# Attention probabilities times values in a fused block: four-pass fp32 products replaced by two fp32r passes for all four heads

## The chip, the cores and the metric

The kernel runs on 1 core of one Trainium2 chip. The metric is the device time of one execution in microseconds (us). The kernel before takes 900.56 us, the median of 3 runs (899.28 to 900.87). From here on TensorE, VectorE, ScalarE, GpSimd and the queue of SyncE are also called PE, DVE, ACT, POOL and SP, as in the profile.

## What is computed

One transformer block on 512 tokens of width 1024, all in float32: a mixer of three attention branches, then attention to a memory of 256 rows, then a gated feed-forward part, each added to the residual. Only the mixer matters here:

```python
o_a = _stick_breaking(q_a, k_a, v_a)                 # 4 heads of 64, each with its own k and v
o_b = _dsa_attention(q_b, k_b, v_b, q_idx, k_idx, w_idx)   # 4 heads share k and v; the best 128 keys of an index score
o_c = _nsa_attention(q_c, k_cmp, v_cmp, k_sel, v_sel, k_win, v_win, gates, ...)  # 4 heads share k and v, three softmaxes
g = jax.nn.sigmoid(p['g_merge'].reshape(B, S, 3, D_MODEL))
merged = g[:,:,0]*(o_a @ w_up[0]) + g[:,:,1]*(o_b @ w_up[1]) + g[:,:,2]*(o_c @ w_up[2])
```

Branch c adds a softmax over 31 compressed keys, one over the selected blocks and one over a window (both are plain causal attention at 512 tokens), each times its gate. Branch b masks the scores by the 128 best of a separate index score and then does one softmax.

## The kernel before

**Precision.** TensorE takes float32 operands as they are, or as "fp32r" in one pass. Nearly every product is written with operands split in two fp32r parts: `split` (line 62) makes `hi` with a cast (ScalarE unless told otherwise) and `lo = src - hi` with a subtraction (VectorE unless told otherwise), and `mm3` (lines 94 to 96) adds three passes. A few small products run on whole float32 operands.

**Order of the work.** The program is written in one order, and a scheduler then sets the order in which each engine gets its instructions, by the place in the program and its own estimates. On the chip each engine keeps to that order, and semaphores hold an instruction until its inputs are there. Weights come in pieces of 512 KB through two rings, both loaded by SP's queue: `load_split` in pool `stage` (three `raw` buffers, `hi` on ACT, `lo` on DVE) and `load_fill` in pool `fill` (two buffers, `lo` on POOL). A ring's piece is loaded when its buffer is free.

**Stages.** First the norm, branch a's projections and stick-breaking attention, beside three of the 24 merge gates (`fill_gate`, `merge_gate`: 24 products of 128x512 for a gate of branch 0 or 2, tile `gf`). Then the projections of b and c, rope, the compressed keys and the index score. Then, in the program's order:

- branch c (`o_c`, lines 625 to 632): for each block `i` of 128 queries `cmp_attention` and two times `rows_attention`; 
- the top-k of the index score: 16 rounds for each of three blocks (`topk_rounds`, lines 615 and 616), on VectorE alone, then the three instructions of line 632 that turn the scores into a mask;
- branch b (`o_b`): `rows_attention` with that mask, so its blocks 1 to 3 can't start before line 632;
- the other five gates of branch 0, `merge_up(0, "a")`, the gates of branch 2, `merge_up(2, "c")`, half of the gates of branch 1, and the rest of the block.

The scheduler puts gates and `merge_up` products between the attention's instructions on TensorE, and rounds of the top-k between those on VectorE.

**One product of probabilities and values** (`apply_v`, lines 561 to 568) takes 128 keys of four heads: four PE transposes of the probabilities into one PSUM bank, one copy to SBUF as float32 (tile `pt`; ACT in branch c, DVE in branch b), and `pair` (line 101): two float32 products, each with the 64 value columns as stationary operand and two heads (256 columns) as moving operand, the first into partitions 0 to 63 and the second into 64 to 127 of `av`. There are 34 such blocks: 4 + 10 + 10 in branch c and 10 in branch b. After each query block the PSUM result is split into `o_hi` and `o_lo` (ACT and DVE, 128x256).

Of the kernel before, what the change touches and what calls it, by code (L numbers as in the profile page):

```python
# [26 lines left out]
def block_kernel(ctx: ExitStack, tc: tile.TileContext, A, out, dbg=None):  # L27
# [16 lines left out]
    cst = const.tile([P, 1408], F32, name="cst")  # L44
    nc.scalar.preload_act_table_set("natural_log_exp_and_others")
    ident = cst[:, 0:128]
    causal = cst[:, 384:896]
    cmpb = cst[:, 896:1024].rearrange("p (h n) -> p h n", n=32)
    rope_t = cst[:, 1024:1536 - 128].rearrange("p (t c d) -> p t c d", t=3, d=32)
# [96 lines left out]
    def cc(c):  # L146
        return slice(c * P, (c + 1) * P)
# [157 lines left out]
    nc.sync.dma_start(cst[:, 128:], A["cst"][:, 128:])  # L305
    nc.vector.memset(fixed[:, 3, :].bitcast(F32), -1.0)
    nc.vector.tensor_copy(fixed[:, 0:3, :], cst[:, 0:384].rearrange("p (a b) -> p a b", b=128))
    flush()
    w0_st.close()

# [118 lines left out]
    vc = bc.tile([32, 64], F32, name="vc")  # L429
# [68 lines left out]
    def compressed(hid):  # L498
        hs = cw.tile([P, 512], F32, name="rel", bufs=2)
        v, t = hs[0:32, 0:256], hs[0:32, 256:512]  # L500
        nc.scalar.copy(v, hid[0:32].rearrange("p a b -> p (a b)"))
        nc.vector.tensor_mul(t, v, v)
        nc.vector.tensor_scalar(t, t, 0.044715, 1.0, op0=ALU.mult, op1=ALU.add)
        nc.vector.tensor_mul(t, t, v)
        nc.scalar.activation(t, t, AF.Exp, scale=-1.5957691216057308)
        nc.vector.tensor_scalar(t, t, 1.0, None, op0=ALU.add)
        nc.vector.reciprocal(t, t)
        nc.vector.tensor_mul(v, v, t)
        tp = ps.tile([P, 512], F32, name="ps")
# [60 lines left out]
    def rows_attention(i, q, k, v, bias, gate, o_ps, first, last, eng=nc.scalar):  # L570
        n = (i + 1) * P
        pr = mq.tile([P, 4, 512], F32, name="pr", bufs=2)
        nm = mq.tile([P, 4], F32, name="nm", bufs=2)
        den = mq.tile([P, 4], F32, name="den", bufs=2)
        for h in range(4):
            st = gm_ps.tile([P, 512], F32, name="gm")
            scores(st[:, :n], q[:, h, cc(i)], [t[:, 0:n] for t in k])
            nc.vector.tensor_tensor_reduce(pr[:, h, :n], st[:, :n], bias, -1.0, 3e38, ALU.add, ALU.min, nm[:, h:h + 1])
            nc.scalar.activation(pr[:, h, :n], pr[:, h, :n], AF.Exp, bias=nm[:, h:h + 1], scale=-1.0, accum_out=den[:, h:h + 1])
        sc = mq.tile([P, 4], F32, name="sc", bufs=2)  # L580
        nc.vector.reciprocal(sc, den)
        if gate is not None:
            nc.vector.tensor_mul(sc, sc, gate)
        for h in range(4):
            if eng is nc.scalar:
                nc.scalar.activation(pr[:, h, :n], pr[:, h, :n], AF.Copy, scale=sc[:, h:h + 1])
            else:
                nc.vector.tensor_scalar(pr[:, h, :n], pr[:, h, :n], sc[:, h:h + 1], None, op0=ALU.mult)
        for j in range(i + 1):
            apply_v(o_ps, v[:, j, :], pr[:, :, cc(j)], first and j == 0, last and j == i, eng=eng)  # L590

    def cmp_attention(i, o_ps, first, last):
        s = mq.tile([P, 4, 32], F32, name="cs")
# [12 lines left out]
        sc = mq.tile([P, 4], F32, name="sc", bufs=2)
        nc.vector.reciprocal(sc, den)
        nc.vector.tensor_mul(sc, sc, gates[:, i, 0::3])
        nc.vector.tensor_mul(s, s, sc.unsqueeze(2).to_broadcast([P, 4, 32]))
        apply_v(o_ps, vc, s, first, last, k=32)  # L610

    def topk_rounds(i, n):
        for _ in range(n):
            m8 = mq.tile([P, 8], F32, name="m8", bufs=3)
            nc.vector.max(m8, score[i])
            nc.vector.match_replace(score[i], m8, score[i], -3e38)

    o_c = o_pair("c", mq)
    for i in range(NT):
        o_ps = av_ps.tile([P, 2, P], F32, name="av")  # L620
        cmp_attention(i, o_ps, True, False)
        rows_attention(i, qc, ksel, vs["vsel"], causal_bias(i), gates[:, i, 1::3], o_ps, False, False)
        rows_attention(i, qc, kwin, vs["vwin"], causal_bias(i), gates[:, i, 2::3], o_ps, False, True)
# [7 lines left out]
    for i in range(1, NT):  # L631
        nc.vector.tensor_scalar(score[i], score[i], -2e38, NEG, op0=ALU.is_gt, op1=ALU.mult)
    o_b = o_pair("b", op)
    for i in range(NT):
        o_ps = av_ps.tile([P, 2, P], F32, name="av")
        rows_attention(i, qb, kb, vs["vb"], score[i] if i else causal_bias(0), None, o_ps, True, True, nc.vector)
        split(o_b[0][:, :, cc(i)], o_b[1][:, :, cc(i)], o_ps, scale=0.5)
    dump("o_b", o_b[0].bitcast(F32))
    for f in range(early_g, NK):
        fill_gate(0, f)  # L640
# [240 lines left out]
def constants():  # L881
    import numpy as np

    c = np.zeros((128, 1408), np.float32)
    i = np.arange(128)
    c[:, 0:128] = np.eye(128, dtype=np.float32)
    c[:, 128:256] = np.where(i[:, None] >= i[None, :], -1.0, 0.0)
    c[:, 256:384] = np.where(i[:, None] >= i[None, :], NEG, 0.0)
    c[:, 768:896] = np.where(i[None, :] > i[:, None], NEG, 0.0)
    n = np.arange(32)  # L890
    for t in range(4):
        q = t * 128 + i
        c[:, 896 + 32 * t:928 + 32 * t] = np.where((16 * n[None, :] + 31 <= q[:, None]) & (n[None, :] < 31), 0.0, NEG)
# [32 lines left out]
```

## Time and profile before

| | |
|---|---|
| median of 3 runs | 900.56 us (899.28 to 900.87) |
| the profiled execution itself | 898.28 us |
| its span, first to last instruction | 896.5 us |
| PE / PE weight load / DVE / ACT / POOL busy | 856.3 / 731.7 / 507.8 / 411.5 / 140.7 us |
| mean granted clock of TensorE | 0.994 |
| branch c with the top-k | 196.7 to 267.0 us |
| branch b | 267.0 to 300.8 us |

Matmuls are pipelined: one is listed with a length of 0.40 us while the next starts 0.23 us later, so the cost of a product is read from start to start. VectorE's instructions overlap by some 0.08 us in the same way. A float32 product appears as two matmuls in the trace, so a block of `pair` is four of them. A row with x12 merges twelve instructions that follow each other.

### The profile page before, as it was taken

The numbers are of one execution on the slowest core, as the hardware profiler recorded it, in microseconds if no ns is written. First come the engines' busy times: TensorE is split into PE (matmuls) and PEld (weight loads), VectorE is DVE, ScalarE is ACT, GpSimd is POOL, SyncE is SP. The second block draws the span as 40 slices with busy tenths as digits, with TensorE's granted clock in tenths as the row PEclk, the third lists the DMA queues.
The fourth block names the chain that finished last, engine by engine and source line by source line (L and its number), as shares of the span: only waits on it lengthen the run. The fifth ranks groups of instructions, "written<-read, shape, count | busy, mean of one in ns | idle before, by whom it ended". The sixth has DMA issues, their size and how long they took to land.

```text
span 896.5 us, 13084 instructions
## 1 busy us (share of the span) xinstructions
PE 856.3 (96%) x5012; PEld 731.7 (82%) x5012; DVE 507.8 (57%) x1155; ACT 411.5 (46%) x779; POOL 140.7 (16%) x116
## 2 busy tenths in 40 slices
PE   5999999899989999999989999999999999999995
PEld 5987899787757788978878979988888888888884
DVE  4456378799998305676677758643443334322226
ACT  6487545557774224544654545432322333211123
POOL 4021232302211347430232010000000000000002
PEclk9999999999999999999999999999999999999998
DMA  9340124510210334558446514642333332333312
GB/s 323 85 110 24 43 58 119 141 48 24 70 26 24 95 94 141 187 174 246 125 150 199 165 49 142 187 142 94 97 102 105 97 94 94 118 94 95 99 42 94
DMA packets 93710, 99.00 MB, mean 110 GB/s; under 512 B 4656, under 2 KB 81616, under 8 KB 93648
## 3 DMA queue, kind: packets, MB, share of 16 engines
q1 hardware_dynamic: 91568, 92.75, 34.0%
q10 hardware_dynamic: 2080, 5.42, 1.9%
q8 instruction: 39, 0.64, 0.3%
q14 instruction: 23, 0.19, 0.1%
HBM read 96.06 MB, written 2.10 MB: 109 GB/s over the span
## 4 chain that ended last, share of the span: by engine, by line
PE 85%; DVE 7%; ACT 4%; issue 2%; DMA 1%; POOL 0%; ACTq 0%; DVEq 0%; POOLq 0%
PE wo L95 9%; PE wo L96 9%; PE wo L94 9%; PE gf L94 6%; PE gf L95 6%; PE gf L96 6%; PE ff L94 4%; PE ff L95 4%; PE ff L96 4%; PE gm L94 3%; PE gm L95 3%; PE gm L96 3%; PE y L96 2%; PE y L94 2%; PE y L95 2%; PE av L101 2%
## 5 line engine op out<-in xcount | busy, mean ns | idle before, releaser
L58 ACT CAST whi<-raw 128x1024 fp32r<-128x1024 f32 (+1 forms) x167 | 174.8, 1048 | 292.4 <-PE y L96 78.9
L66 DVE TENSOR_TENSOR wlo<-raw,whi 128x1024 fp32r<-128x1024 f32 (+1 forms) x131 | 164.1, 1255 | 211.2 <-ACT whi L58 210.9
L66 POOL TENSOR_TENSOR wlo<-raw,whi 128x1024 fp32r<-128x1024 f32 x36 | 88.9, 2474 | 312.9 <-ACT whi L58 267.1
L95 PE MATMUL wo<-ut_lo,whi 128*128 128x256 f32 (+1 forms) x320 | 105.2, 329 | 0.0
L96 PE MATMUL wo<-ut_hi,wlo 128*128 128x256 f32 (+1 forms) x320 | 104.6, 327 | 0.0
L94 PE MATMUL wo<-ut_hi,whi 128*128 128x256 f32 (+1 forms) x320 | 104.4, 326 | 0.0
L96 PE MATMUL gf<-ut_hi,wlo 128*128 128x512 f32 (+1 forms) x192 | 69.8, 363 | 0.0
L94 PE MATMUL gf<-ut_hi,whi 128*128 128x512 f32 (+1 forms) x192 | 69.3, 361 | 0.0
L95 PE MATMUL gf<-ut_lo,whi 128*128 128x512 f32 (+1 forms) x192 | 69.3, 361 | 0.0
L94 PE MATMUL ff<-ut_hi,whi 128*128 128x512 f32 (+1 forms) x192 | 67.9, 354 | 0.0
L95 PE MATMUL ff<-ut_lo,whi 128*128 128x512 f32 (+1 forms) x192 | 67.9, 354 | 0.0
L96 PE MATMUL ff<-ut_hi,wlo 128*128 128x512 f32 (+1 forms) x192 | 67.9, 354 | 0.0
L95 PEld LDWEIGHTS wo<-ut_lo,whi 128*128 128x128 f32 x320 | 60.9, 190 | 6.2 <-issue 1.0
L94 PEld LDWEIGHTS wo<-ut_hi,whi 128*128 128x128 f32 x320 | 60.8, 190 | 5.8 <-issue 0.7
L96 PEld LDWEIGHTS wo<-ut_hi,wlo 128*128 128x128 f32 x320 | 60.8, 190 | 5.6 <-issue 0.4
L875 POOL TENSOR_TENSOR ut_hi<-ut_hi,ut_lo 128x512 f32<-128x512 f32 x4 | 5.0, 1276 | 367.0 <-ACT ut_hi L874 367.0
L94 PE MATMUL gm<-whi,ut_hi 128*128 128x256 f32 (+1 forms) x160 | 47.4, 296 | 0.0
L95 PE MATMUL gm<-wlo,ut_hi 128*128 128x256 f32 (+1 forms) x160 | 46.4, 290 | 0.0
L96 PE MATMUL gm<-whi,ut_lo 128*128 128x256 f32 (+1 forms) x160 | 46.3, 289 | 0.0
L96 PEld LDWEIGHTS gf<-ut_hi,wlo 128*128 128x128 f32 x192 | 36.2, 188 | 5.6 <-issue 1.2
L95 PEld LDWEIGHTS gf<-ut_lo,whi 128*128 128x128 f32 x192 | 36.2, 188 | 5.4 <-issue 0.8
L94 PEld LDWEIGHTS gf<-ut_hi,whi 128*128 128x128 f32 x192 | 36.2, 188 | 5.3 <-issue 0.8
(329 smaller groups left out, 2027.7 us busy)
## 6 DMA issues: line engine op xcount, KB each, us to landing
raw<-in_w_ffn_in_dram SPq DMA_DIRECT2D x56, 512.0 KB, 3.6
raw<-in_w_in_dram SPq DMA_DIRECT2D x46, 512.0 KB, 3.9
raw<-in_w_ffn_out_dram SPq DMA_DIRECT2D x22, 512.0 KB, 3.5
raw<-in_w_out_dram SPq DMA_DIRECT2D x16, 512.0 KB, 3.6
raw<-in_w_up_dram SPq DMA_DIRECT2D x8, 512.0 KB, 4.0
xt<-in_x_dram SPq DMA_DIRECT2D x4, 512.0 KB, 9.0
raw<-in_w_mem_kv_dram SPq DMA_DIRECT2D x4, 512.0 KB, 3.8
raw<-in_w_mem_q_dram SPq DMA_DIRECT2D x4, 512.0 KB, 3.8
```

Source lines behind the costliest of these rows:

```text
L58: nc.scalar.copy(dst, src)
L66: (lo_eng or nc.vector).tensor_sub(dst_lo, src, dst_hi.bitcast(F32))
L94: nc.tensor.matmul(dst, lh, rh, start=first, stop=False, skip_group_check=True)
L95: nc.tensor.matmul(dst, lh, rl, start=False, stop=False, skip_group_check=True)
L96: return nc.tensor.matmul(dst, ll, rh, start=False, stop=last, skip_group_check=True).ins
L101: nc.tensor.matmul(dst[64 * x:64 * x + 64], lhs[x], rhs[x], start=first, stop=last, skip_group_check=True)
L875: nc.gpsimd.tensor_mul(yo[:, n], yo[:, n], gain[:, n])
```

## The change

1. `apply_v` turns the transposed probabilities into two fp32r parts (`pt_hi` by ACT, `pt_lo` by DVE, both from PSUM, 128x512) instead of one float32 copy, in both branches. The values stand as 128 stationary columns, their high part beside their low part, and two products, `pt_hi` and `pt_lo`, each 512 columns wide (four heads), add into one PSUM bank. So partitions 0 to 63 of `av` hold the high value part's result and 64 to 127 the low part's.
2. `fold` adds the two halves after each query block: two ACT copies (64x256) into a `raw` buffer of the `stage` ring, two DVE additions (64x256), then the split into `o_hi` and `o_lo` from SBUF.
3. `two_parts` splits the values of the three row attentions once (128x256, ACT and DVE each).
4. `cmp_attention` has no buffer of its own any more: it takes one of the two `pr` buffers of the row attentions, GpSimd clears columns 32 to 127 of it, and its transposes and product run over 128 keys.
5. The table of constants is laid out anew, and the rope tables are loaded later, into a pool of the projections. The program's order of attention and gates is as before.

```diff
-    def apply_v(o_ps, v, src, first, last, k=P, eng=nc.scalar):
+    def apply_v(o_ps, v, src, first, last):
         tp = ps.tile([P, 4, P], F32, name="ps")
         for h in range(4):
-            nc.tensor.transpose(tp[0:k, h, :], src[:, h, :], ident)
-        pt = mq.tile([P, 4, P], F32, name="pt", bufs=3)
-        copy(eng, pt[0:k], tp[0:k])
-        pair(o_ps, [v, v], [pt[0:k, x::2, :] for x in range(2)], first, last)
+            nc.tensor.transpose(tp[:, h, :], src[:, h, :], ident)
+        pt = [mq.tile([P, 4, P], F32R, name=n, bufs=2) for n in ("pt_hi", "pt_lo")]
+        split(pt[0], pt[1], tp)
+        for x in range(2):
+            nc.tensor.matmul(o_ps, v.rearrange("p a d -> p (a d)"), pt[x].rearrange("p h q -> p (h q)"),
+                             start=first and x == 0, stop=last and x == 1, skip_group_check=True)
+
+    def fold(o, i, o_ps):
+        ov = o_ps.rearrange("p (a b q) -> p a b q", a=2, b=2)
+        hi, lo = (t[:, :, cc(i)] for t in o)
+        t = stage.tile([P, WT], F32, name="raw", bufs=3)[:, 0:2 * P].rearrange("p (a q) -> p a q", a=2)
+        top, bot = slice(0, 64), slice(64, 128)
+        nc.scalar.copy(t[top], ov[bot, :, 0, :])
+        nc.scalar.copy(t[bot], ov[top, :, 1, :])
+        nc.vector.tensor_add(t[top], ov[top, :, 0, :], t[top])
+        nc.vector.tensor_add(t[bot], ov[bot, :, 1, :], t[bot])
+        split(hi, lo, t, scale=0.5)
...
     def cmp_attention(i, o_ps, first, last):
-        s = mq.tile([P, 4, 32], F32, name="cs")
+        pr = mq.tile([P, 4, 512], F32, name="pr", bufs=2)
+        s = pr[:, :, 0:32]
+        nc.gpsimd.memset(pr[:, :, 32:128], 0.0)
...
-        apply_v(o_ps, vc, s, first, last, k=32)
+        apply_v(o_ps, vc, pr[:, :, 0:128], first, last)
...
+    def two_parts(v):
+        t = mq.tile([P, NT, 2, 64], F32R, name="v2", bufs=2)
+        split(t[:, :, 0, :], t[:, :, 1, :], v)
+        return t
+
+    vsel, vwin = two_parts(vs["vsel"]), two_parts(vs["vwin"])
...
-        o_ps = av_ps.tile([P, 2, P], F32, name="av")
+        o_ps = av_ps.tile([P, 512], F32, name="av")
...
-        split(o_c[0][:, :, cc(i)], o_c[1][:, :, cc(i)], o_ps, scale=0.5)
+        fold(o_c, i, o_ps)
...
+    rope_t = pw.tile([P, 3, NT, 32], F32, name="rope_t")
+    nc.sync.dma_start(rope_t, A["cst"][:, 1024:1408].rearrange("p (t c d) -> p t c d", t=3, d=32))
```

How the scheduler's order changes, at three places.

VectorE in branch c, in the last query block. `score_1246` to `score_1248` (before) and `score_1250` to `score_1252` (changed) are the three index scores, `m_...` the eight maxima of a round. Before:

```order
L615 MAX m_3298<-score_1248 128x8
L615 MAX m_3301<-score_1246 128x8
L616 MATCH_REPLACE score_1248<-m_3298,score_1248 128x512
L616 MATCH_REPLACE score_1246<-m_3301,score_1246 128x256
L581 RECIPROCAL sc<-den 128x4
L615 MAX m_3304<-score_1247 128x8
L583 TENSOR_TENSOR sc<-sc,gates 128x4
L615 MAX m_3307<-score_1248 128x8
```

Changed:

```order
L637 MATCH_REPLACE score_1252<-m_3356,score_1252 128x512
L65 TENSOR_TENSOR pt_lo<-ps,pt_hi 128x512 x2
L636 MAX m_3359<-score_1250 128x8
L636 MAX m_3362<-score_1251 128x8
L65 TENSOR_TENSOR pt_lo<-ps,pt_hi 128x512
L600 RECIPROCAL sc<-den 128x4
L637 MATCH_REPLACE score_1250<-m_3359,score_1250 128x256
L65 TENSOR_TENSOR pt_lo<-ps,pt_hi 128x512
```

All 24 `pt_lo` subtractions of branch c, all eight additions of its `fold`, four `o_lo` (before: three) and two of the `two_parts` stand between the first instruction of the compressed attention and the first mask instruction; of the 96 top-k instructions all but one stand ahead of the mask, as all did before.

VectorE just ahead of the attention (`wlo` is a weight piece of `load_split`; the one here belongs to a gate of branch 1, which is multiplied behind the attention). Before:

```order
L66 TENSOR_TENSOR wlo<-raw,whi 128x1024
L66 TENSOR_TENSOR stk<-t_2570,stk 128x4x64
L66 TENSOR_TENSOR kc_lo<-ps,kc_hi 128x32
L522 COPY vc<-ps 32x64
L615 MAX m_3184<-score_1246 128x8
```

Changed:

```order
L65 TENSOR_TENSOR stk<-t_2576,stk 128x4x64
L65 TENSOR_TENSOR kc_lo<-ps,kc_hi 128x32
L65 TENSOR_TENSOR vc<-ps,vc 32x64
L636 MAX m_3269<-score_1250 128x8
```

Two such pieces (the other is half of `w_up` of branch c) stood among the last 15 instructions ahead of the attention; both now come after it.

TensorE at the end of the attention (`vb` before and `v_3418` now are branch b's values, `o_hi`/`o_lo` beside `whi`/`wlo` are `merge_up`, `ut_hi`/`ut_lo` are gates). Before:

```order
L101 MATMUL av<-pt,vb 64x256 x4
L96 MATMUL gf<-ut_hi,wlo 128x512
L94 MATMUL gf<-ut_hi,whi 128x512
L565 MATMUL ps<-cst,pr 128x128 x4
L95 MATMUL gf<-ut_lo,whi 128x512
L565 MATMUL ps<-cst,pr 128x128 x3
L101 MATMUL av<-pt,vb 64x256 x6
L565 MATMUL ps<-cst,pr 128x128 x5
L96 MATMUL gf<-ut_hi,wlo 128x512
L94 MATMUL gf<-ut_hi,whi 128x512
L101 MATMUL av<-pt,vb 64x256 x8
```

Changed:

```order
L574 MATMUL av<-pt_hi,v_3418 128x512
L95 MATMUL gf<-o_hi,wlo 128x512
L93 MATMUL gf<-o_hi,whi 128x512
L94 MATMUL gf<-o_lo,whi 128x512
L95 MATMUL gf<-o_hi,wlo 128x512
L574 MATMUL av<-pt_lo,v_3418 128x512
L93 MATMUL gf<-o_hi,whi 128x512
L94 MATMUL gf<-o_lo,whi 128x512
```

28 of the 512-column products (13 of gates, 6 of `merge_up(0)`, 9 of `merge_up(2)`) that stood ahead of the last probability-value product stand behind it now. From branch c's first score to branch b's first score TensorE's order holds 128 of them (110 before), and from there to the last probability-value product 30 (70 before).

## Rows read from the trace of the kernel before

**Rows 1.** The page: busy time of each engine.

```profile
PE 856.3 (96%) x5012; PEld 731.7 (82%) x5012; DVE 507.8 (57%) x1155; ACT 411.5 (46%) x779; POOL 140.7 (16%) x116
```

**Rows 2.** Busy time by stretch: start:end, length, each engine's busy us, granted clock, DMA.

```profile
core 0: us, PE busy (x) PEld busy (x) DVE busy (x) ACT busy (x) POOL busy (x), PEclk, DMA share, GB/s
180.20:196.70 16.50, 16.50 (x125) 15.21 (x125) 15.22 (x42) 9.52 (x20) 0.00 (x0) 1.00 0.19 48
196.70:267.00 70.30, 67.92 (x402) 48.70 (x401) 67.92 (x261) 54.66 (x137) 11.94 (x5) 1.00 0.13 36
267.00:300.80 33.80, 31.05 (x171) 22.59 (x167) 26.09 (x78) 13.27 (x38) 4.75 (x2) 0.95 0.16 45
300.80:896.50 595.70, 577.40 (x3142) 494.09 (x3142) 287.71 (x450) 224.23 (x344) 79.80 (x46) 0.99 0.40 124
```

**Rows 3.** Timeline of VectorE, end of the top-k: start, length, instruction.

```profile
266.41 0.68 DVE L616 MATCH_REPLACE8 score<-m,score 128x512 f32<-128x512 f32 x1
267.00 0.55 DVE L632 TENSOR_SCALAR score<-score 128x256 f32<-128x256 f32 x2
```

**Rows 4.** Groups of VectorE from 190 to 310 us: busy us, mean ns, idle before.

```profile
L60 DVE COPY pt<-ps 128x512 f32<-128x512 f32 x10 | 6.6, 687 | 3.1 <-PE av L101 2.2 <-PE ps L565 0.9
L388 DVE SCALAR_TENSOR_TENSOR g<-g,gf 128x512 f32<-128x512 f32 x8 | 5.5, 682 | 2.4 <-PE gf L96 2.4
L69 DVE SCALAR_TENSOR_TENSOR o_lo<-av,o_hi 128x256 fp32r<-128x256 f32 x8 | 3.4, 421 | 2.2 <-ACT o_hi L68 2.0
```

**Rows 5.** Timeline of VectorE in the first norm: a 128x512 subtraction from PSUM.

```profile
10.17 0.68 DVE L66 TENSOR_TENSOR ut_lo<-ps,ut_hi 128x512 fp32r<-128x512 f32 x1
10.77 1.21 DVE L66 TENSOR_TENSOR wlo<-raw,whi 128x1024 fp32r<-128x1024 f32 x1
```

**Rows 6.** Timeline of VectorE ahead of the attention.

```profile
190.50 1.21 DVE L66 TENSOR_TENSOR wlo<-raw,whi 128x1024 fp32r<-128x1024 f32 x1
191.63 0.41 DVE L66 TENSOR_TENSOR stk<-t,stk 128x256 fp32r<-128x256 f32 x1
```

**Rows 7.** Timeline of TensorE around three probability-value products.

```profile
234.46 0.39 PE L96 MATMUL gf<-ut_hi,wlo 128*128 128x512 f32 x1
234.78 1.52 PE L101 MATMUL av<-pt,vsel 128*64 128x256 f32 x12
236.22 0.50 PE L94 MATMUL gf<-ut_hi,whi 128*128 128x512 f32 x1
236.56 0.40 PE L95 MATMUL gf<-ut_lo,whi 128*128 128x512 f32 x1
236.79 0.40 PE L96 MATMUL gf<-ut_hi,wlo 128*128 128x512 f32 x1
```

**Rows 8.** Busy time in pieces of 2.5 us around the dip of the granted clock.

```profile
265.00:267.50 2.50, 1.50 (x11) 0.51 (x7) 2.50 (x8) 0.81 (x2) 0.36 (x1) 1.00 0.36 82
267.50:270.00 2.50, 1.29 (x5) 1.29 (x6) 2.23 (x11) 1.27 (x6) 0.00 (x0) 0.73 0.43 128
270.00:272.50 2.50, 2.50 (x10) 2.12 (x10) 2.01 (x11) 1.48 (x7) 0.00 (x0) 0.59 0.00 0
```

**Rows 9.** Timeline of TensorE inside that dip.

```profile
270.16 0.63 PE L95 MATMUL gf<-o_lo,whi 128*128 128x512 f32 x1
270.59 0.41 PE L292 MATMUL gm<-kb_hi,qi 128*128 128x256 f32 x1
```

**Rows 10.** Groups of ScalarE from 190 to 310 us.

```profile
L58 ACT COPY pt<-ps 128x512 f32<-128x512 f32 x20 | 10.7, 586 | 4.3 <-PE ps L565 3.3 <-PE ps L293 0.9
L68 ACT ACTIVATE o_hi<-av 128x256 fp32r<-128x256 f32 x8 | 3.1, 384 | 9.8 <-PE av L101 9.8
```

**Rows 11.** Timeline of TensorE at the last probability-value product.

```profile
298.69 2.10 PE L101 MATMUL av<-pt,vb 128*64 128x256 f32 x16
300.72 0.50 PE L95 MATMUL gf<-ut_lo,whi 128*128 128x512 f32 x1
```

**Rows 12.** Group of GpSimd from 196 to 345 us.

```profile
L66 POOL TENSOR_TENSOR wlo<-raw,whi 128x1024 fp32r<-128x1024 f32 x15 | 35.8, 2388 | 123.4 <-ACT whi L58 110.4 <-PE gf L96 13.0
```

More of the change, by code (lines that the diff above doesn't have):

```diff
@@ L43, in block_kernel @@
     utp = pool(ctx, "ut")
-    cst = const.tile([P, 1408], F32, name="cst")
+    cst = const.tile([P, 768], F32, name="cst")
     nc.scalar.preload_act_table_set("natural_log_exp_and_others")
     ident = cst[:, 0:128]
-    causal = cst[:, 384:896]
-    cmpb = cst[:, 896:1024].rearrange("p (h n) -> p h n", n=32)
-    rope_t = cst[:, 1024:1536 - 128].rearrange("p (t c d) -> p t c d", t=3, d=32)
+    causal = cst[:, 128:640]
+    cmpb = cst[:, 640:768].rearrange("p (h n) -> p h n", n=32)
     eps = const.tile([P, 1], F32, name="eps")
@@ L304, in block_kernel @@
             project_chunk(c, 256, w_a[8 * i:8 * i + 8], post)
-    nc.sync.dma_start(cst[:, 128:], A["cst"][:, 128:])
+    tri = pw.tile([P, 2, 128], F32, name="tri")
+    nc.sync.dma_start(tri, A["cst"][:, 768:1024].rearrange("p (a b) -> p a b", b=128))
+    nc.sync.dma_start(cst[:, 128:], A["cst"][:, 128:768])
     nc.vector.memset(fixed[:, 3, :].bitcast(F32), -1.0)
-    nc.vector.tensor_copy(fixed[:, 0:3, :], cst[:, 0:384].rearrange("p (a b) -> p a b", b=128))
+    nc.vector.tensor_copy(fixed[:, 0, :], ident)
+    nc.vector.tensor_copy(fixed[:, 1:3, :], tri)
     flush()
@@ L428, in block_kernel @@
     kc = k_pair(bc, "kc", 32)
-    vc = bc.tile([32, 64], F32, name="vc")
+    vc = bc.tile([P, 2, 64], F32R, name="vc")
+    nc.gpsimd.memset(vc.bitcast(F32), 0.0)
     score = [None] + [bc.tile([P, (i + 1) * P], F32, name=f"score{i}") for i in range(1, NT)]
@@ L521, in compressed @@
         split(kc[0], kc[1], res[:, 0:32])
-        nc.vector.tensor_copy(vc, res[0:32, 64:128])
+        split(vc[0:32, 0, :], vc[0:32, 1, :], res[0:32, 64:128])
     project([(1732, 256)], 4, post_g2)
@@ L589, in rows_attention @@
         for j in range(i + 1):
-            apply_v(o_ps, v[:, j, :], pr[:, :, cc(j)], first and j == 0, last and j == i, eng=eng)
+            apply_v(o_ps, v[:, j, :, :], pr[:, :, cc(j)], first and j == 0, last and j == i)
     def cmp_attention(i, o_ps, first, last):
-        s = mq.tile([P, 4, 32], F32, name="cs")
+        pr = mq.tile([P, 4, 512], F32, name="pr", bufs=2)
+        s = pr[:, :, 0:32]
+        nc.gpsimd.memset(pr[:, :, 32:128], 0.0)
         st = ps.tile([P, 4, P], F32, name="ps")
@@ L616, in topk_rounds @@
             nc.vector.match_replace(score[i], m8, score[i], -3e38)
+    def two_parts(v):
[3 more added lines that the diff above has]
+    vsel, vwin = two_parts(vs["vsel"]), two_parts(vs["vwin"])
     o_c = o_pair("c", mq)
     for i in range(NT):
-        o_ps = av_ps.tile([P, 2, P], F32, name="av")
+        o_ps = av_ps.tile([P, 512], F32, name="av")
         cmp_attention(i, o_ps, True, False)
-        rows_attention(i, qc, ksel, vs["vsel"], causal_bias(i), gates[:, i, 1::3], o_ps, False, False)
-        rows_attention(i, qc, kwin, vs["vwin"], causal_bias(i), gates[:, i, 2::3], o_ps, False, True)
-        split(o_c[0][:, :, cc(i)], o_c[1][:, :, cc(i)], o_ps, scale=0.5)
+        rows_attention(i, qc, ksel, vsel, causal_bias(i), gates[:, i, 1::3], o_ps, False, False)
+        rows_attention(i, qc, kwin, vwin, causal_bias(i), gates[:, i, 2::3], o_ps, False, True)
+        fold(o_c, i, o_ps)
     dump("o_c", o_c[0].bitcast(F32))
@@ L633, in block_kernel @@
     o_b = o_pair("b", op)
+    vb = two_parts(vs["vb"])
     for i in range(NT):
-        o_ps = av_ps.tile([P, 2, P], F32, name="av")
-        rows_attention(i, qb, kb, vs["vb"], score[i] if i else causal_bias(0), None, o_ps, True, True, nc.vector)
-        split(o_b[0][:, :, cc(i)], o_b[1][:, :, cc(i)], o_ps, scale=0.5)
+        o_ps = av_ps.tile([P, 512], F32, name="av")
+        rows_attention(i, qb, kb, vb, score[i] if i else causal_bias(0), None, o_ps, True, True, nc.vector)
+        fold(o_b, i, o_ps)
     dump("o_b", o_b[0].bitcast(F32))
@@ L886, in constants @@
     c[:, 0:128] = np.eye(128, dtype=np.float32)
-    c[:, 128:256] = np.where(i[:, None] >= i[None, :], -1.0, 0.0)
-    c[:, 256:384] = np.where(i[:, None] >= i[None, :], NEG, 0.0)
-    c[:, 768:896] = np.where(i[None, :] > i[:, None], NEG, 0.0)
+    c[:, 768:896] = np.where(i[:, None] >= i[None, :], -1.0, 0.0)
+    c[:, 896:1024] = np.where(i[:, None] >= i[None, :], NEG, 0.0)
+    c[:, 512:640] = np.where(i[None, :] > i[:, None], NEG, 0.0)
     n = np.arange(32)
@@ L892, in constants @@
         q = t * 128 + i
-        c[:, 896 + 32 * t:928 + 32 * t] = np.where((16 * n[None, :] + 31 <= q[:, None]) & (n[None, :] < 31), 0.0, NEG)
+        c[:, 640 + 32 * t:672 + 32 * t] = np.where((16 * n[None, :] + 31 <= q[:, None]) & (n[None, :] < 31), 0.0, NEG)
     inv = np.float32(10000.0) ** (-np.arange(0, 64, 2, dtype=np.float32) / np.float32(64))
```

## Prediction

> **What bounds the kernel now.** On the page TensorE is busy 856.3 us and VectorE 507.8 [rows 1], which makes TensorE look like the one limit. So I next read the busy times by stretch [rows 2], because an edit in the attention is worth what that stretch makes of it. In the 70.3 us of branch c with the top-k, VectorE is busy 67.92 us, exactly as long as TensorE: both are full, and VectorE has 2.4 us to spare. In branch b (33.8 us) TensorE has 31.05 and VectorE 26.09. Behind it TensorE is busy for 577.4 of 595.7 us. Then I looked at what ends branch c: the mask instruction at 267.00 stands on VectorE right behind the last replacement of the top-k [rows 3], and branch b's blocks 1 to 3 cannot begin before it. In a stretch with two full engines, work taken from one gains nothing when work is given to the other, and this change does that.
>
> **What it does to TensorE.** Three blocks of the old float32 product run from 234.78 to 236.22, so one takes 0.48 us [rows 7]. A 512-column fp32r product takes 0.23 (236.56 to 236.79), and the new block is two, 0.46: over 34 blocks 0.7 us. More comes from the borders: before a float32 group the gap is 0.32 and behind it 0.34 instead of 0.23 [rows 7], 0.2 a group, and TensorE's old order has 20 groups: 4 us. So at most 4.7 us leave TensorE. Twelve transposes more stand ahead of branch b's first score; at no more than the 0.23 of a product four times as wide they are 2.8 us at most, and TensorE's waits found below cover them. The Trainium skill, "FP8 and Floating Point Precision", section "TensorE Precision Notes", says that true fp32 takes 4 passes through the array. By that rule, an estimate, one half of the old block is 4 x 256 columns at 2.4 GHz, 0.43 us, and both halves in turn 0.85, so that 34 blocks would give back 13 us; the 0.48 us of the row, which covers both halves, does not bear that out, and the sum goes by the row.
>
> **What it does to VectorE in branch c.** From the order, between the first compressed-attention instruction and the mask:
> - 24 subtractions `pt_lo` are new (the copies they go with were ScalarE's). The nearest row is a subtraction of the same 128x512 shape from PSUM: 0.68 long, and the next instruction starts 0.60 after it [rows 5]. 24 x 0.60 = 14.4 us.
> - 8 `fold` additions of 64x256; the nearest row is `o_lo`, 256 elements a partition, 0.42 long [rows 4], less the same 0.08 overlap 0.34: 2.7 us.
> - one `o_lo` and two `two_parts` more, 0.34 each: 1.0 us.
> - one replacement moves behind the mask: 267.00 less 266.41 [rows 3], -0.6 us.
>
> Sum +17.5 us on an engine that has 2.4 free. Ahead of the stretch two `wlo` leave, 1.13 us each from start to start (190.50 to 191.63) [rows 6]; VectorE is busy 15.22 of the 16.5 us there, but so is TensorE [rows 2], so I take 2.0 of the 2.3. The mask then comes at 267.0 - 2.0 + 17.5 = 282.5 if VectorE waits as little as before. It now also waits for ScalarE's cast before each subtraction, and the compressed attention waits for a `pr` buffer and for GpSimd's clearing, which is queued behind `wlo` pieces of 2.4 us [rows 12]: 0 to 5 us, I take 2, since the top-k rounds between them still fill most gaps, as they do now. Mask at 284.5. TensorE cannot set a longer time: 67.9 us, plus 18 more 512-column products (4.1) and the transposes (2.8), is 75 us at most, against VectorE's 85.4.
>
> **Branch b.** On VectorE the ten copies become ten subtractions (0.69 against 0.68, nothing). Two `merge_up` instructions (-1.2) and four `o_lo` (-1.4) go behind the stretch; six additions (+2.0), one `two_parts` (+0.3) and the replacement (+0.6) come in: 26.1 + 0.3 = 26.4 us. TensorE loses 40 of its 70 products of 512 columns, 9.2 us. So the stretch, 33.8 us now, is no shorter than 27, and no longer than the 34 it takes with the larger TensorE load; I take 30, since some of VectorE's 7.7 idle us stood behind those products (`pt` waited 3.1 and `g` 2.4 [rows 4]).
>
> **Behind the attention.** The last probability-value product ends at 300.7 now [rows 11] and would end at 284.5 + 30 = 314.5, 13.7 us later. 28 products, 28 x 0.23 = 6.4 us, that ran before it now come after it. From there TensorE is full, so both are added.
>
> **What costs nothing.** ScalarE gets ten casts of 0.59 and sixteen copies of at most 0.38 [rows 10] over both stretches, 12 us, beside 67.9 busy of 104 [rows 2]; uncovered, they would stand in the chain of a block, which the 5 us above bound. The rope table leaves SP's queue when branch a has ended and is read some microseconds later; its 0.2 MB is less than half of a weight piece, and I count 0. On SP's queue the two `w_up` pieces of branch c now wait for `raw` buffers that `fold` holds, and hold later pieces back; four gates' pieces stand ahead of them, 24 x 0.23 = 5.5 us of TensorE each, which cover it. Without that cover the wait of a piece would show, and one gate's 5.5 us bounds it.
>
> **The sum.** -2.0 + 17.5 + 2.0 - 3.8 + 6.4 = +20.1 us. The profiled execution took 898.28, 2.28 under the median of the runs, so it would become 918.4, and the median 900.56 + 20.1 = 920.7. With no added waits and branch b at 27 it is +15.1 (915.7); with 5 us of waits and 34 it is +27.1 (927.7).
>
> **Rivals.**
> - *TensorE's clock falls.* Around 265 to 270 us, with TensorE busy 1.50 and 1.29 of 2.5 us, the granted clock went to 0.73 and 0.59, that is to the lower of its two levels (1.2 instead of 2.4 GHz) for most of 5 us [rows 8], and a 512-column product took 0.43 us from start to start [rows 9]. In the changed branch c TensorE would be busy 75 of 87 us at most, so dips are likely. If it spent more than a fifth of that at the lower level, its 75 us (x 1.87 there) would pass VectorE's 87 and set the time: a third gives 75 x 1.29 = 97, 10 us more, 930. Against: at 1.50 of 2.5 us, 60%, it was still granted 1.00 [rows 8], and 75 of 87 is 86%. The Trainium skill, "TensorE: Matmul & The Clock Gate", section "What's actually happening", makes this the rule, a TensorE that goes idle falls back to half rate; the dip agrees with it, at 0.59.
> - *TensorE alone sets the pace (faster).* If the top-k were mere filling and its end did not hold up branch b, the 17.5 us would vanish in gaps and the 4.7 us of TensorE would come off: 895.9. That needs more than 17.5 us of VectorE idle ahead of the mask, and rows 2 show 2.4; for it speaks only that TensorE is just as busy.
> - *Only part is exposed.* If the mask came no later than TensorE's own additions make it (4.1 + 2.8 - 3 of borders, about 4 us), the sum is -2 + 4 - 3.8 + 6.4 = +4.6: 905.2. It would take most subtractions in places where VectorE now waits. In its mild form the change can't be told from none.
> - *That the attention's place before the gates is not changed* is settled by the order: the 28 products did move.
>
> **How the numbers follow.** The forecast, VectorE sets branch c, has 0.72 and its own range 916 to 928; the clock 0.10 at 927 to 940; partly exposed 0.10 at 900 to 910; faster 0.08. The time predicted is the forecast's, 920.7. The range reaches up to 932, into the clock's case, and down to 910, so that the two low cases and a bit of the clock, just under 0.2, are left out. About 0.2% (1.8 us) is what a measurement can tell from no change: faster 0.08 (the second rival), same 0.03 (part of the third), slower 0.89.
>
> **What would show it.** Right: VectorE at 95% or more from 195 to about 285 with the mask near 284; TensorE with waits for `pt_lo` or for VectorE's maxima there, in all some 20 us more idle than the 5 of the two stretches now; subtractions of 0.68 on VectorE; the last product near 314, and from there to the end some 602 us. Wrong: a mask before 275, or TensorE busy as fully as now through branch c; products of 0.43 us over long parts of it mean the first rival.

## The result and the profile after

The changed kernel takes 924.01 us, the median of 4 runs (923.13 to 925.62); the kernel before took 899.92 (898.47 to 900.87) beside it. The ratio is 1.0271, 95% interval 1.025 to 1.0292: slower, inside the predicted range and 3.3 us above the predicted time. The profiled execution has a span of 923.8 us against 896.5.

The page of the changed kernel, busy times and the slices of three engines and the clock, stands against [rows 1]:

```profile
PE 864.4 (94%) x4944; PEld 741.7 (80%) x4944; DVE 533.6 (58%) x1199; ACT 423.3 (46%) x809; POOL 141.2 (15%) x121
PE   5999999899974899999999999999999999999995
DVE  4466388799989820847678676653443344322226
PEclk9999999999986999999999999999999999999998
```

VectorE has 25.8 us more, TensorE 8.1. TensorE was 96% busy and is 94%. Its row has one hole, the 12th to 14th slice (254 to 323 us), which read 7, 4 and 8; in the deepest of them, the 13th (277 to 300 us), VectorE's row reads 9. By stretch (start:end, length, busy us of PE, PEld, DVE, ACT, POOL, granted clock), with the end of TensorE's branch c and the mask as borders, to be laid beside [rows 2]:

```profile
195.60:276.90 81.30, 73.74 (x360) 55.72 (x359) 76.63 (x261) 57.83 (x146) 13.24 (x8) 0.96 0.12 33
276.90:288.40 11.50, 0.00 (x0) 0.00 (x0) 11.44 (x35) 1.15 (x3) 0.00 (x0) 0.58 0.00 0
288.40:319.30 30.90, 25.70 (x119) 19.34 (x120) 26.82 (x82) 17.88 (x49) 2.41 (x1) 0.88 0.16 52
319.30:923.80 604.50, 585.35 (x3171) 500.54 (x3169) 295.18 (x460) 229.90 (x353) 80.50 (x47) 0.99 0.41 127
```

Branch c with the top-k took 70.3 us and now takes 92.8, the first two rows together. VectorE is busy for 88.07 of them, 95%. TensorE is busy for 73.74, has finished its last product of branch c at 276.9, and then does nothing at all until VectorE is through. The span's 27.3 us are -1.1 (the stretch starts at 195.6 instead of 196.7), +22.5 (branch c), -2.9 (branch b, 30.9 instead of 33.8) and +8.8 (behind the attention, 604.5 instead of 595.7).

TensorE's timeline over the hole (start, length, instruction, in brackets the idle time and what ended it), and of VectorE's the last maximum ahead of the mask, the first mask instruction, and the first row maximum behind the mask:

```profile
274.63 0.78 PE L574 MATMUL av<-pt_lo,v 128*128 128x512 f32 x1
275.65 0.50 PE L574 MATMUL av<-pt_hi,v 128*128 128x512 f32 x1 [0.25 <-ACT pt_hi L57]
276.38 0.50 PE L574 MATMUL av<-pt_lo,v 128*128 128x512 f32 x1 [0.23 <-DVE pt_lo L65]
290.62 0.47 PE L291 MATMUL gm<-kb_hi,qi 128*128 128x128 f32 x1 [13.74 <-DVE nm L597]
```

```profile
287.77 0.68 DVE L636 MAX8 m<-score 128x8 f32<-128x512 f32 x1
288.38 0.27 DVE L659 TENSOR_SCALAR score<-score 128x256 f32<-128x256 f32 x1
290.26 0.29 DVE L597 CUSTOM_DVE_ANT_0 pr<-gm,cst 128x128 f32<-128x128 f32 x1
```

The mask instruction, at 267.00 before [rows 3], starts at 288.38. TensorE's next score product needs a PSUM buffer that VectorE's row maximum of branch b's first block sets free (290.26), and that maximum is queued behind the top-k and the mask: 13.74 us of waiting, in one piece. The first block itself needs no mask; it is VectorE's order that holds it up. No run moved this maximum ahead of the top-k. Where VectorE's time went, by groups of the stretch from 195.6 to 288.4 (busy us, mean ns, idle before):

```profile
L65 DVE TENSOR_TENSOR pt_lo<-ps,pt_hi 128x512 fp32r<-128x512 f32 x24 | 15.9, 683 | 1.9 <-ACT pt_hi L57 1.9
L621 DVE TENSOR_SCALAR nm<-nm 128x4 f32<-128x4 f32 x4 | 2.2, 548 | 0.0
L586 DVE TENSOR_TENSOR raw<-av,raw 64x256 f32<-64x256 f32 x4 | 1.7, 427 | 0.1
L585 DVE TENSOR_TENSOR raw<-av,raw 64x256 f32<-64x256 f32 x4 | 1.6, 411 | 0.0
```

The 24 new subtractions are by far the largest group that was not there before. The second row is a surprise, told at the end.

### The profile page after: what moved, and what is told of

Same layout as the page of the kernel before. It is cut to its first block, busy times and chain, and to the rows that moved or that the text cites. A ratio compares the mean times of both kernels' runs of the same rounds, so it can differ in the third digit from the quotient of the medians.

```text
span 923.8 us, 13054 instructions
## 1 busy us (share of the span) xinstructions
PE 864.4 (94%) x4944; PEld 741.7 (80%) x4944; DVE 533.6 (58%) x1199; ACT 423.3 (46%) x809; POOL 141.2 (15%) x121
## 4 chain that ended last, share of the span: by engine, by line
PE 77%; DVE 13%; ACT 4%; DMA 3%; issue 2%; POOL 0%; ACTq 0%; DVEq 0%; SPq 0%; POOLq 0%
PE wo L94 8%; PE wo L95 8%; PE wo L93 8%; PE gf L93 5%; PE gf L94 5%; PE gf L95 5%; PE ff L94 4%; PE ff L93 4%; PE ff L95 4%; PE gm L93 2%; PE gm L94 2%; PE gm L95 2%; PE y L93 2%; PE y L95 2%; PE y L94 2%
## 5 line engine op out<-in xcount | busy, mean ns | idle before, releaser
L93 PEld LDWEIGHTS ff<-ut_hi,whi 128*128 128x128 f32 x192 | 36.3, 189 | 5.0
L95 PEld LDWEIGHTS ff<-ut_hi,wlo 128*128 128x128 f32 x192 | 36.3, 189 | 5.0
L94 PEld LDWEIGHTS ff<-ut_lo,whi 128*128 128x128 f32 x192 | 36.3, 189 | 4.9
```

What stands on the lines that cost most here:

```text
L93: nc.tensor.matmul(dst, lh, rh, start=first, stop=False, skip_group_check=True)
L94: nc.tensor.matmul(dst, lh, rl, start=False, stop=False, skip_group_check=True)
L95: return nc.tensor.matmul(dst, ll, rh, start=False, stop=last, skip_group_check=True).ins
```

## The experiments

Theory V is the prediction's: VectorE's sum of work sets the time of the mask, and TensorE loses what it waits for. Against it stood W, that the time goes on TensorE's own new product blocks and their dependences, whatever VectorE does, and T, the prediction's first rival, that the clock is the loss. All were timed in 3 rounds beside the kernel before; the medians of the kernel before were 899.64 for the first four, then 898.0, 899.07 and 899.3.

| run | edit | median us | ratio, 95% | mask at |
|---|---|---|---|---|
| changed kernel | none | 924.01 | 1.0271 (1.025 to 1.0292) | 288.4 |
| 1 | changed, no low part | 905.19 | 1.0057 (1.0037 to 1.0077) | 271.0 |
| 3 | changed, 8 rounds of top-k | 898.96 | 0.999 (0.9981 to 1.0) | 244.3 |
| 4 | before, 8 rounds of top-k | 896.09 | 0.9969 (0.9953 to 0.9985) | 234.9 |
| 5 | before, 20 subtractions added | 911.96 | 1.0139 (1.0123 to 1.0154) | 281.8 |
| 2a | changed, gates and a merge moved ahead | 920.96 | 1.0245 (1.0222 to 1.0268) | 286.7 |
| 2b | before, gates and a merge moved ahead | 900.54 | 1.0031 (1.0019 to 1.0043) | 267 |
| 6 | changed, low part on GpSimd | 930.66 | 1.0359 (1.0341 to 1.0377) | 283.7 |
| 7 | 6 and 2a together | 928.01 | 1.0324 (1.0303 to 1.0346) | 286.2 |
| 8 | changed, 8 gates ahead, no merge | 904.42 | 1.0061 (1.0046 to 1.0076) | 285.5 |
| 11 | changed, 9 gates ahead, no merge | 898.29 | 0.9993 (0.9983 to 1.0003) | 286.7 |
| 9 | changed, 13 gates ahead, no merge | 909.12 | 1.0115 (1.01 to 1.013) | 286.2 |
| 10 | before, 8 gates ahead, no merge | 893.74 | 0.9943 (0.9926 to 0.9959) | 266.3 |

### Less and more work on VectorE (runs 1, 3, 4, 5)

Run 1 takes the low part of the probabilities away from the changed kernel, on VectorE and on TensorE:

```diff
-        pt = [mq.tile([P, 4, P], F32R, name=n, bufs=2) for n in ("pt_hi", "pt_lo")]
-        split(pt[0], pt[1], tp)
-        for x in range(2):
+        pt = [mq.tile([P, 4, P], F32R, name=n, bufs=2) for n in ("pt_hi",)]
+        nc.scalar.copy(pt[0], tp)
+        for x in range(1):
...
```

> The changed kernel without the low part of the probabilities: no pt_lo subtraction and one product a block instead of two; the low parts are left out of the result. Theory V (VectorE's sum of work sets when the top-k ends, and TensorE waits for the mask): 24 x 0.60 = 14.4 us leave VectorE ahead of the mask, so the mask comes at 272 to 275 instead of 288.4, branch b is 2 to 5 us shorter, the time is 902 to 909. Rival T (TensorE at its lower clock sets branch c): TensorE has less to do and idles more, the clock is no better, 915 or more. Rival W (the chain cast, subtraction, product of each block holds things up, not VectorE's sum): as V, this run does not tell them apart.

Runs 3 and 4 leave out half the rounds of the top-k, in the changed kernel and in the one before:

```diff
-    for r in range(16):
+    for r in range(8):
```

> The changed kernel with 8 rounds of the top-k instead of 16, so branch b keeps more wrongly chosen keys out: half of the top-k is left out. V: some 26 us leave VectorE ahead of the mask, TensorE becomes the one that sets branch c, the change costs nothing any more and the 4.7 us of TensorE show: 893 to 899, below the kernel before with the same 8 rounds. W: every block still has its cast and subtraction in line, 910 or more. T: 910 or more.

> The kernel before with 8 rounds of the top-k instead of 16 (half of the top-k is left out). V: TensorE is as full as VectorE there, so freeing VectorE gives little: 895 to 900. W and T say the same; it is the partner of the changed kernel with 8 rounds.

Run 5 gives the kernel before one subtraction of the same shape, whose result nobody reads, beside each copy in branch c:

```diff
         copy(eng, pt[0:k], tp[0:k])
+        if k == P and eng is nc.scalar:
+            dz = mq.tile([P, 4, P], F32, name="dz")
+            nc.vector.tensor_sub(dz, tp, pt)
```

> The kernel before, with a subtraction of 128x512 from PSUM on VectorE added beside each of the 20 copies that ScalarE makes in branch c; nobody reads its result. V: 20 x 0.60 = 12 us on an engine with 2.4 us to spare; the mask moves from 267 to 276 to 279 and the time is 907 to 913. W: no product waits for it, under 903. T: under 903.

Run 5 is the cleanest: TensorE's work is the old one, and 20 instructions on VectorE alone cost 12.3 us (911.96 less 899.64), 0.62 each, close to the start-to-start time of 0.60 [rows 5]. The wait appears in the old kernel just where the change put it. TensorE's waits from 188 to 330 us (us in all, times, longest), in run 5:

```profile
PE gm L292 <- DVE nm L581: 12.9, 4, 12.1
PE av L101 <- ACT pt L58: 2.4, 4, 0.7
PE ps L565 <- ACT pr L589: 0.5, 1, 0.5
```

W and T, which expected under 903, can't explain that run. Run 1 brings back 18.8 of the change's 24.1 us, but it takes products off TensorE as well, so it does not price the subtractions alone. Its mask came at 271.0, earlier than the 272 to 275 expected: 17.4 us for 24 subtractions, of which 14.4 are their price, and VectorE's waits for `pt_hi` (1.9 us in the changed kernel) and the long `nm` instruction (1.5, told at the end) went with them.

Runs 3 and 4 show the change when VectorE has room: 898.96 against 896.09, 2.9 us instead of 24. Run 3's expectation, that the changed kernel would be the faster of the two, did not come true, if by little: the single times overlap (897.66 to 899.45 and 894.64 to 900.20). So one term of the prediction, TensorE's saving, finds no support. With 8 rounds the granted clock is 1.00 in both kernels through the attention, and the pages of the two read, run 3 first, then run 4:

```profile
PE 854.5 (95%) x4944; PEld 734.0 (82%) x4944; DVE 511.6 (57%) x1127; ACT 423.8 (47%) x809; POOL 141.0 (16%) x121
```

```profile
PE 853.3 (96%) x5012; PEld 728.3 (82%) x5012; DVE 487.2 (55%) x1083; ACT 410.7 (46%) x779; POOL 140.6 (16%) x116
```

TensorE is busy 1.2 us longer in the changed kernel, by the page's count, not some microseconds less. With half of the top-k left out the change shows no gain that could be given back.

### Work for TensorE to do while it waits (runs 2a, 2b, 8 to 11)

If TensorE's idle time is the loss, products that need nothing from VectorE's queue should fill it. Run 2a wrote the later gates of branch 0, their merge and one gate of branch 2 ahead of branch b's loop, and 2b did so in the kernel before with one gate more:

```diff
+    for f in range(early_g, NK):
+        fill_gate(0, f)
+    merge_up(0, "a", load_fill, gf_ps)
+    for f in range(1):
+        fill_gate(2, f)
     o_b = o_pair("b", op)
...
-    for f in range(early_g, NK):
-        fill_gate(0, f)
-    merge_up(0, "a", load_fill, gf_ps)
-    for f in range(NK):
+    for f in range(1, NK):
         fill_gate(2, f)
```

> The changed kernel, with the later gates of branch 0, their merge and one gate of branch 2 written ahead of branch b's loop, so that 61 products of 512 columns stand on TensorE between branch c's last product and branch b's first score. At 0.23 us each that is 14 us of work that needs nothing from VectorE, where TensorE stood idle for 13.7 us. Theory V (VectorE's sum of work sets when the mask is there, TensorE stands idle, and what it loses is that idle time and the lower clock after it): 908 to 915 us, mask still at 287 to 291, clock 1.00 where it was 0.50. Theory W (the time goes on TensorE's own longer product blocks): 920 to 926, the gates moved change nothing. Theory T (the clock alone is the loss, some 4 to 7 us): 916 to 920.

> The kernel before with the same move (one gate of branch 2 more). There branch b's first score waited little for the mask. Theory V: within 0.4% of the kernel before, 897 to 903. Theory W: the same. If the move gains over 5 us here too, what it gains in the changed kernel isn't an answer to the change.

2b took 0.3% more than the kernel before (900.54 against 898.0), within what was expected. 2a missed: 3 us of gain, not 9 to 16. Taken alone, its 920.96 lies in W's range; its timeline of TensorE shows another reason:

```profile
274.65 0.51 PE L574 MATMUL av<-pt_lo,v 128*128 128x512 f32 x1 [0.23 <-DVE pt_lo L65]
288.95 0.79 PE L93 MATMUL gf<-o_hi,whi 128*128 128x512 f32 x1 [13.79 <-DVE g L390]
289.54 0.63 PE L94 MATMUL gf<-o_lo,whi 128*128 128x512 f32 x1
289.97 0.63 PE L95 MATMUL gf<-o_hi,wlo 128*128 128x512 f32 x1
```

The expectation called these products free of VectorE, and they are not: `merge_up` multiplies each product into the gate on VectorE (line 390), which empties one of the two `gf` buffers, and that instruction stood behind the top-k as the row maximum had. The same wait had a new name. The gates' products are emptied by ScalarE (line 375), and their weights are split by ScalarE and GpSimd. So runs 8, 11 and 9 move the five later gates of branch 0 and three, four or all eight of branch 2, and leave the merge behind branch b; run 10 does that with three in the kernel before:

```diff
+    for f in range(early_g, NK):
+        fill_gate(0, f)
+    for f in range(3):
+        fill_gate(2, f)
     o_b = o_pair("b", op)
...
-    for f in range(early_g, NK):
-        fill_gate(0, f)
     merge_up(0, "a", load_fill, gf_ps)
-    for f in range(NK):
+    for f in range(3, NK):
         fill_gate(2, f)
```

> The changed kernel with the five later gates of branch 0 and three of branch 2 written ahead of branch b, but without branch 0's merge, whose sums on VectorE held up the earlier run with moved gates. 60 more products of 512 columns lie among branch c's work and 12 behind it, 72 in all or 16.5 us, and ScalarE and GpSimd alone serve them; TensorE was idle for 19 us of that stretch. Theory V (VectorE's sum of work sets the mask, and what is lost is TensorE's idle time): mask still at 287 to 291, TensorE's idle time ahead of the mask under 8 us, 906 to 912 us. If the products delay what VectorE reads: mask at 292 to 300, 912 to 920. Theory W (the longer product blocks on TensorE): 920 to 926.

> The changed kernel with nine gates ahead of branch b (the five later ones of branch 0, four of branch 2): 24 products more than with eight, 5.5 us, for TensorE's last idle stretch of 7.2 us ahead of the mask. Theory V: mask unchanged at 285 to 289, that idle stretch under 3 us, 898 to 902 us. If the gate's transfers and splits, or branch 2's merge later, wait for weights as with thirteen gates (6.9 us): 903 to 909. Theory V also says that it stays above the kernel before with eight gates moved (893.7).

> As the run before, with all eight gates of branch 2 ahead of branch b: 192 more products (44 us) between branch c's first instruction and branch b's masked rows, more than the 19 us that TensorE was idle there. Theory V: TensorE sets the pace of that stretch, idle under 4 us in all, mask at 305 to 320, 902 to 909 us. Theory W: 920 to 926.

> The kernel before with the first of these moves: 72 more products ahead of its mask, where TensorE was idle for about 2 us. Every theory: mask some 14 us later, 896 to 902 us, since TensorE had next to nothing to fill. If it gains over 5 us, the move is worth something by itself and what it gains in the changed kernel is no answer to the change.

Run 8 falls to 904.42, a little below its range of 906 to 912, and run 11 to 898.29, level with the kernel before. Their masks are still late, at 285.5 (287 to 291 was expected) and 286.7. W, which expected 920 to 926 for run 8, falls with it. TensorE's wait for `nm` ahead of branch b shrinks from 13.74 us to 7.16 and to 2.09; the timelines of run 8 and run 11:

```profile
287.12 0.47 PE L291 MATMUL gm<-kb_hi,qi 128*128 128x128 f32 x1 [7.16 <-DVE nm L597]
```

```profile
288.29 0.33 PE L291 MATMUL gm<-kb_hi,qi 128*128 128x128 f32 x1 [2.09 <-DVE nm L597]
```

The same 150 us, 190 to 340, of four kernels (busy us of PE, PEld, DVE, ACT, POOL, then the granted clock): the changed kernel, run 8, run 11, run 10.

```profile
190.00:340.00 150.00, 125.57 (x606) 96.02 (x605) 128.09 (x399) 90.75 (x222) 24.37 (x13) 0.92 0.19 54
```

```profile
190.00:340.00 150.00, 138.59 (x684) 109.23 (x683) 127.56 (x397) 94.98 (x228) 32.53 (x16) 0.97 0.26 72
```

```profile
190.00:340.00 150.00, 143.62 (x714) 112.95 (x714) 128.66 (x401) 96.48 (x230) 34.96 (x17) 0.99 0.26 74
```

```profile
190.00:340.00 150.00, 148.46 (x801) 110.85 (x800) 102.90 (x356) 84.22 (x201) 37.10 (x16) 1.00 0.22 64
```

VectorE's column hardly moves between the first three; TensorE's does, and the time follows it: 13.0 us more busy and 19.6 less in all from the changed kernel to run 8, then 5.0 more and 6.1 less to run 11, then 4.8 more and 4.6 less to run 10. The first step gives more than the busy time it fills; the granted clock comes back in it from 0.92 to 0.97, and the mask comes 2.9 us earlier. What each of the two gave was not separated.

Run 10 means a correction. The expectation said that a gain of over 5 us in the kernel before would make the move worth something by itself, and it gained 5.3, to a time below the expected 896 to 902. Its mask (266.3) did not move either, where some 14 us were expected. TensorE's busy time from 190 to 340 us rose from 144.87 to 148.46 in it, so the kernel before had some idle time to fill as well. Of the 19.6 us of run 8, 5.3 are to be had without the change, and the others, some 14, answer to the change. With eight gates in both, the change costs 10.7 us (904.42 against 893.74); the best changed version, run 11, is still 4.6 above run 10. **Run 10, the kernel before with eight gates ahead, beats both kernels**: 0.9943 of the kernel before.

Run 9 shows the far end. With thirteen gates TensorE has no long wait left ahead of branch b: from 190 to 340 us its longest is 1.8. The products delay branch b, its last value product comes at 337.5 instead of 315.9 in run 8, a new wait stands behind it, and the time, 909.12, is just above the expected 902 to 909. TensorE's waits of run 9 from 340 to 400:

```profile
PE gm L93 <- ACT whi L57: 6.9, 1, 6.9
PE gm L93 <- DVE g L390: 1.1, 1, 1.1
PE gm L93 <- ACT mg_hi L57: 0.7, 2, 0.5
```

It is the first product of branch 2's merge, at 347.97: its weights' transfer was issued at 341.94, and ScalarE had still to make their high part. None of the other runs shows that wait. Its mask (286.2) missed the expected 305 to 320: the extra products did not hold VectorE up at all.

### The low part on another engine (runs 6 and 7)

Run 6 takes the subtraction off VectorE: ScalarE copies the transposed block to SBUF, GpSimd subtracts. Run 7 adds run 2a's move to it.

```diff
-        split(pt[0], pt[1], tp)
+        nc.scalar.copy(src, tp)
+        nc.scalar.copy(pt[0], src)
+        nc.gpsimd.tensor_sub(pt[1], src, pt[0].bitcast(F32))
```

> The changed kernel, with the low part subtracted by GpSimd: ScalarE copies the transposed block out of PSUM and rounds it, GpSimd subtracts. VectorE loses 34 subtractions of 0.68 us, 24 of them ahead of the mask (16 us); ScalarE gains 34 copies of about 0.59 us. Theory V: mask at 270 to 276, 904 to 912 us. If ScalarE's or GpSimd's longer chain sets branch c's pace in VectorE's place: 912 to 925, with TensorE's products waiting for the low part on GpSimd. Theory W: 920 to 926.

> Both edits together: the low part on GpSimd, and the 61 products ahead of branch b. If VectorE's end and TensorE's idle time are all that was lost: 896 to 906 us, TensorE's idle time ahead of branch b's first score under 2 us. If the two edits mend the same microseconds: no better than the better one of the two alone.

Run 6, at 930.66, is above every range that was expected, W's too, and run 7, at 928.01, is no better than run 2a alone (920.96). The mask came only 4.7 us earlier in run 6, not 12 to 18, and branch b's last value product came at 336.8 instead of 319.0. Groups of run 6 over the whole span, and waits from 190 to 345 us:

```profile
L574 POOL TENSOR_TENSOR pt_lo<-pr,pt_hi 128x512 fp32r<-128x512 f32 x34 | 44.1, 1322 | 68.6 <-ACT pt_hi L573 45.5 <-DVE m L638 19.0 <-PE gm L292 4.0
L572 ACT COPY pr<-ps 128x512 f32<-128x512 f32 x34 | 18.8, 590 | 14.4 <-PE ps L570 12.8 <-DVE sc L604 1.5
```

```profile
PE av L576 <- POOL pt_lo L574: 15.4, 27, 1.3
DVE pr L599 <- POOL pt_lo L574: 6.8, 6, 1.6
```

A subtraction that took VectorE 0.68 us takes GpSimd 1.32, with a copy of 0.59 ahead of it in the same chain. TensorE waits for it 27 times, 15.4 us in all, and VectorE 6.8 us, because the probabilities' buffer is not free before GpSimd has read it. Up to the mask VectorE is busy for 77.5 of 88.1 us, so it waits for 10.6 us, where it waited for 4.7.

And it did not get all of its time back: 14.4 us of subtractions left it, and its busy time fell by 10.6 (from 88.07). Six small instructions of the compressed attention that began while GpSimd was subtracting took 0.98 to 2.16 us, where they take 0.16 to 0.29 otherwise, 6.4 us more in all. One of them, with GpSimd's row beside it:

```profile
216.46 2.16 DVE L628 TENSOR_SCALAR den<-den 128x4 f32<-128x4 f32 x1
```

```profile
216.23 2.37 POOL L65 TENSOR_TENSOR wlo<-raw,whi 128x1024 fp32r<-128x1024 f32 x1 [2.69 <-ACT whi L57]
```

This doesn't speak against V. Two things took back what VectorE had gained, the longer chain through each block and these drawn-out instructions, and no run separates them.

## Why the prediction was right, step by step

- **What bounds branch c.** As argued from [rows 2]: with both engines full, work given to VectorE showed in full. VectorE is 95% busy up to the mask, and run 5 prices a subtraction near what the prediction took, 0.60: 20 cost 12.3 us, 0.62 each. Run 1 agrees, less cleanly: without the 34 of both branches, 20.4 us at 0.60, and half of their products, 18.8 come back. TensorE was idle for 24.3 of the 123.7 us of both branches, where it had been idle for 5.1; some 20 more were forecast. What held it up was narrower than the prediction said: the row maximum of branch b's first block, which needs no mask but stands behind it on VectorE, and not only blocks 1 to 3.
- **VectorE's sum of +17.5 us, and 2.0 of waits.** The stretch became 22.5 us longer instead of 19.5. VectorE's busy time rose by 20.2 (88.07 less 67.92), so the sum was 2.7 short; its idle time rose by 2.4 (4.7 instead of 2.4), near the 2.0 taken. Of the 2.7, 1.5 are the one `nm` instruction told of below. The rest is spread; no row singles it out.
- **The earlier start, -2.0.** It was -1.1: of the 2.3 us of `wlo` half came through. Together these put the mask at 288.4 instead of 284.5.
- **Branch b at 30 us.** 30.9. The last value product ended at 319.3, forecast 314.5, 3.9 of the difference being the mask's.
- **Behind the attention, +6.4.** It was +8.8, the second term that was too small. TensorE's busy time there rose by 8.0 (585.35 less 577.40) where 28 products were priced at 6.4, and 0.8 is more idle time. Between 450 and 500 us the granted clock is 0.97, where the kernel before has 1.00; what sets that off was not tried.
- **TensorE's saving of up to 4.7 us.** It was not in the sum, and rightly: runs 3 and 4 show no saving at all. The 4 us of it that came from borders have no support either: in the changed kernel a gap of about 0.3 us is still found behind transposes, here 0.32 from 234.57 to 234.89, so it didn't belong to the old product alone.

```profile
234.19 0.63 PE L570 MATMUL ps<-cst,pr 128*128 128x128 f32 x4
234.57 0.47 PE L94 MATMUL gf<-ut_lo,whi 128*128 128x512 f32 x1
234.89 0.39 PE L95 MATMUL gf<-ut_hi,wlo 128*128 128x512 f32 x1
```

- **The clock rival.** TensorE's clock did fall to its lower level, 0.50 in the whole of 280 to 290 us, but as a consequence: it stood still. The Trainium skill, "TensorE: Matmul & The Clock Gate", section "What's actually happening", says that an idle TensorE falls back to half rate; the trace agrees, with 0.58 over the 11.5 idle us. It didn't set the length of branch c, since TensorE ended 11.5 us ahead of the mask.
- **The other two rivals.** Both needed idle time on VectorE: TensorE alone setting the pace wanted more than 17.5 us of it, the partly exposed case a mask some 4 us later than before. The mask came 21.4 us later.
- **The forecast's size.** -1.1, +22.5, -2.9 and +8.8 make 27.3 us of span, against 20.1 predicted. The medians differ by less, 24.1: the profiled execution after was the slowest of its four (925.62), and the one before, 898.28, was faster than the three timed ones (899.28 to 900.87). The steps were short by 0.9 (the start), 3.0 (branch c), 0.9 (branch b) and 2.4 (behind the attention), 7.2 us of span; 3.2 of that (27.3 less 24.1) belongs to the two executions, not to the kernels. So the 3.3 us by which the median missed flatter the terms: every one of them was short, and none made up for another.

## What to carry to other kernels

Where two engines are full in the same stretch, price an edit on the one that gets work, by start-to-start time, and expect nothing from relief on the other. To fill an idle engine, follow the filling to the engine that empties its buffers: products whose results pass through the late engine wait with it (run 2a), those emptied elsewhere fill the hole (runs 8 and 11). And try the filling on the kernel before too: here it was worth 5.3 us there, more than the 4.7 that the prediction allowed TensorE at most.

## What was not expected of the hardware

**One short VectorE instruction lasted as long as GpSimd's.** An instruction on 4 elements a partition, 0.16 or 0.17 us in its other places, took 1.70 in the changed kernel. Timelines of VectorE and of GpSimd:

```profile
227.32 1.70 DVE L621 TENSOR_SCALAR nm<-nm 128x4 f32<-128x4 f32 x1
228.93 0.54 DVE L597 CUSTOM_DVE_ANT_0 pr<-gm,cst 128x384 f32<-128x384 f32 x1
```

```profile
226.61 2.39 POOL L65 TENSOR_TENSOR wlo<-raw,whi 128x1024 fp32r<-128x1024 f32 x1 [7.20 <-ACT whi L57]
```

It ends at 229.02, and GpSimd's subtraction, which began before it, at 229.00. The same is seen elsewhere. In the changed kernel three `o_lo` from 322.06 took 3.08 us, one of them 2.41, beside a `wlo` on GpSimd from 321.79 to 324.20, where one alone takes 0.42; they now read `raw` and `o_hi`, both in SBUF, where the kernel before read `av` in PSUM and never took over 0.43 for one of this size. In run 10 the three mask instructions took 2.39 us beside a `wlo` from 265.50 to 267.89; in run 5, with GpSimd idle, the three took 0.89. In run 1 the same `nm` instruction began 1.2 us after GpSimd's `wlo` had ended (at 227.55) and took 0.18, and in run 6, where GpSimd had more to subtract, six instructions were drawn out. The Trainium skill, "SBUF — State Buffer", section "Who interferes with whom", says that VectorE and GpSimd share a pair of ports as an exclusive lock, for VectorE instructions with two SBUF inputs or in a two-port mode; these rows agree, though no row tells which mode an instruction ran in. No run was made to take GpSimd's work away, so it is read from coincidences in time, not shown by an edit of its own. In branch c of the changed kernel it comes to 1.5 us.

**What an idle stretch leaves behind.** In run 2a, after 13.8 idle us, 512-column products start 0.43 us apart from 289.54 to 293.81, ten steps, and 0.23 from 294.17 on. The granted clock (the first number behind GpSimd's busy time) is 0.50 in the first stretch and 1.00 in the next:

```profile
288.90:294.10 5.20, 5.15 (x12) 4.09 (x13) 2.04 (x7) 0.93 (x5) 0.00 (x0) 0.50 0.00 0
294.10:300.00 5.90, 5.90 (x27) 4.87 (x27) 2.92 (x5) 1.35 (x2) 2.40 (x1) 1.00 0.21 59
```

That is 2.0 us lost after the idle time itself (ten steps at 0.43 instead of 0.23). That part of the loss, T's, is there and small.
